# Where the second hidden column's weight sums are computed: in the fill stage, or on three engines in the up stage

## The chip, the cores and the metric

The kernel runs on one core of a Trainium2 chip. The core has TensorE (PE in the profile, with its weight loads as PEld), VectorE (DVE), ScalarE (ACT), GpSimd (POOL) and SyncE (SP), which all run their own instruction queue in order and wait for each other by semaphores. Most loads are issued by SP's queue, most stores by POOL's. The metric is the device time of one execution in microseconds (us). Shown is the median of several runs, and beside it one profiled execution with its trace.

## The reference

One layer of a diffusion backbone, on 1024 latent ("sample") tokens and 128 context ("prompt") tokens of width 1024: a normalised and modulated input goes through a mixer (four GLA heads and four HGRN2 heads, scanned in both directions), an output projection with a gate and a residual, a second norm, and a feed-forward part. The change lies in the first half of the feed-forward part:

```python
def conv_ffn(h, w_up, conv_w, conv_b, w_down, grid):
    u = dw_conv(h @ w_up, conv_w, conv_b, grid)      # 3x3 over the latent grid, width 3 over the prompt
    gate, up = jnp.split(u, 2, axis=-1)
    return (jax.nn.silu(gate) * up) @ w_down
```

`w_up` is 1024 x 5632: 2816 gate channels and 2816 up channels. The outputs are the normed tokens and the final states of the scans.

## The kernel before, in words

*Precision.* Every float32 factor is split into a high part, a copy rounded to `fp32r` made by ScalarE, and a low part, the difference, made by VectorE or GpSimd (`split_lo`, recorded on L69). A product is then three matmuls: high by high, high by low, low by high.

*Stages.* The mixer comes first (to about 724 us). At its end TensorE is filled with the output projection of finished token tiles (L746), whose results go to DRAM (`scr_pre`). Then comes the **fill stage**: the rest of the output projection (`head7` L1486, `heads` L1503), and for each of nine token tiles `mult`, `add`, `square`, `stat` and `norm` (L1411 to L1431), the transposes (L1439, L1460, L1476) and the modulation that makes the feed-forward's token blocks. Then the **up stage** (from about 801 us): 22 hidden columns of 128 gate and 128 up channels each. Then the down product.

*The up product.* For each hidden column c the product of the weights (two rows: gate and up; two halves of the 1024 inputs) with the tokens (two halves of the inputs, two of the tokens) is made by seven block products instead of eight. They need the four weight blocks `11`, `12` (gate), `21`, `22` (up) and four sums of them: `s1` = 21 + 22, `s2` = s1 - 11, `s4` = 12 - s2, `s3` = 11 - 21. A block is 128 x 512. `up(c, p)` (L1921) issues product p: 1 uses `11`, 2 `12`, 3 `s4`, 4 `22`, 5 `s1`, 6 `s2`, 7 `s3`; `up_prompt(c, half)` (L1945) multiplies the prompt with the four blocks themselves. The split weights of all columns live in the tile pair `W` of nine slots, which a search (`plan_slots`, L1690) hands on from column to column. Raw blocks lie in `ra` (`11`, `12`, `21`, `22`) and `sr` (the sums); prompt tokens lie for a while in the last two quarters of `sr`.

From column 2 on, SP loads the raw rows (`load_row`, L1710) a column ahead, GpSimd makes the sums (`weight_sums`, L1732), and ScalarE and GpSimd split them (`split_slots`, L1718). VectorE is left to the convolution of each column (`conv_rows`, L1874, recorded on L1890), which reads the product in PSUM. There are three PSUM tiles `u` of two banks, so a convolution's end sets a later product free.

*Columns 0 and 1 are prepared earlier.* `prepare_up(c)` (L1271) runs for c = 0 and c = 1 behind the mixer: it loads the blocks into the raw buffers, ScalarE copies and VectorE sums and splits, through two `fb` buffers, and GpSimd's queue stores the high and low parts to DRAM (`scr_up`). In the up stage `load_first` (L1763) loads them into `W`.

*Order.* The Tile framework orders each engine's work, and where the text wants an order it writes it by hand: `run(eng, fn)` (L1262) issues `fn` on the engine behind what the last `run` put there. `prepare_up`, the whole fill stage and column 0 go through it, so on VectorE `mult(0)` of the fill stage stands behind the last split of `prepare_up(1)`. The token tiles 0, 1, 4 and 5 are loaded into the raw buffers (`load_xt`, L1391); tile 6's and 7's heads (`load_mh`, L1399) come from DRAM too.

*Tokens in column 0.* While TensorE works on column 0, `prompt_work` (L1797) modulates, copies and splits the prompt, and splits t3; `first_sums` (L1808) makes and splits t4, and adds two products' copies to the gate product, whose convolution starts then.

Of the kernel before, what the change touches and what calls it, by code (L numbers as in the profile page):

```python
# [8 lines left out]
F32 = mybir.dt.float32  # L9
# [3 lines left out]
AF = mybir.ActivationFunctionType  # L13
# [4 lines left out]
P = 128  # L18
# [31 lines left out]
def kernel(ctx: ExitStack, tc: tile.TileContext, ins, outs, stop=None):  # L50
# [46 lines left out]
    scr_up = [[dram.tile([P, 8, 512], F32, name=f"scr_up{c}{x}") for x in "hl"] for c in range(2)]  # L97
    scr_t = [dram.tile([NPAIR, P, 512], F32, name=f"scr_t{i}") for i in range(4)]

    def x_src(t):  # L100
# [1167 lines left out]

    UP0 = ("11", "12", "21", "22", "s1", "s2", "s4", "s3")

    def prepare_up(c):  # L1271

        r = {}
        for row in (1, 2):
            t = rawp.tile([P, 2, 512], F32, name="up0", tag="raw")
            for half in range(2):
                nm = f"{row}{half + 1}"
                r[nm] = t[:, half]
                c0 = (row - 1) * HID + c * P
                nc.sync.dma_start(  # L1280
                    r[nm].rearrange("p (k c) -> p k c", k=4),
                    w_up[half * 512 : (half + 1) * 512, c0 : c0 + P].rearrange("(k p) c -> p k c", p=P),
                )

        def split(nm, place, keep):
            hi = fbp.tile([P, 512], F32R, name="up_hi", tag="fb")
            lo = fbp.tile([P, 512], F32R, name="up_lo", tag="fb") if keep else r[place].bitcast(F32R)
            run("act", lambda: nc.scalar.activation(hi, r[place], AF.Copy))
            run("dve", lambda: split_lo(nc.vector, lo, r[place], hi))
            for i, t in enumerate((hi, lo)):  # L1290
                nc.gpsimd.dma_start(scr_up[c][i][:, UP0.index(nm)], t.bitcast(F32))
# [12 lines left out]
        split("12", "12", True)  # L1304
        in_place("12", "12", "11", ALU.subtract)
        split("s2", "11", False)
        split("s4", "12", False)

    for c in range(2):
        prepare_up(c)  # L1310

    es1.close()
    es_t.close()
# [449 lines left out]
    def load_first(c, nm, dst=None):  # L1763
        for i, x in enumerate("hl"):
            to = dst[x] if dst else W[x][:, SLOT[c][nm]]
            nc.sync.dma_start(flat(to).bitcast(F32), scr_up[c][i][:, UP0.index(nm)])

    def next_weights(c, names):
        if c == 1:
            for nm in names:  # L1770
                load_first(c, nm)
        else:
            split_slots(c, names, nc.gpsimd)

    for nm in ("11", "12"):
        load_first(0, nm, {x: w_slot(0, nm, x) for x in "hl"})
    for nm in ("s1", "s2", "s4", "22", "21", "11", "s3", "12"):
        load_first(0, nm)
    load_row(2, 2)
    load_row(2, 1)  # L1780

    def new_tiles(nm, i):
        for x, j in (("h", 0), ("l", 1)):
# [13 lines left out]
    def prompt_work():  # L1797

        for kt in range(KT):
            modulate_prompt(kt)  # L1800
        copy(0, "p5", u[0][0][:, 512:NS])
        run("act", lambda: nc.scalar.activation(HB["h"]["p"], again["p"], AF.Copy))
        run("dve", lambda: split_lo(nc.vector, HB["l"]["p"], again["p"], HB["h"]["p"]))
        for n in range(2):
            half_hi("t3", n, tmp[n])
            half_lo("t3", n, tmp[n])

    def first_sums():  # L1808

        F = u[0][0]  # L1810
        new_tiles("t4", 1)
        run("dve", lambda: tt(F[:, 0:512], F[:, 0:512], copies["p1"], op=ALU.add))
        for n in range(2):
            token_sum(tmp[2 + n], rb(1, 0, n), tmp[2 + n])
            half_hi("t4", n, tmp[2 + n])
        run("dve", lambda: tt(F[:, 512:NS], F[:, 512:NS], copies["u2"], op=ALU.add))
        for n in range(2):
            half_lo("t4", n, tmp[2 + n])

    token_work()  # L1820
    HB["h"]["p"] = again["late"].tile([P, KT, P], F32R, name="ph", tag="gate")
# [52 lines left out]
    def conv_rows(u, ch, acc, ra=0, rb=NROW):  # L1874

        wc = lambda t: convc[:, t * 44 + ch : t * 44 + ch + 1]
        bc = vcol[:, col["conv_b"] + ch : col["conv_b"] + ch + 1]
        nc.scalar.activation(  # L1878
            acc[:, ra * GRID : rb * GRID], u[:, ra * GRID : rb * GRID], AF.Identity, bias=bc, scale=wc(4)
        )  # L1880
        u3 = u.rearrange("p (r c) -> p r c", c=GRID)
        a3 = acc[:, 0:NS].rearrange("p (r c) -> p r c", c=GRID)
        for dy in (-1, 0, 1):
            for dx in (-1, 0, 1):
                if dy == 0 and dx == 0:
                    continue
                r0, r1 = max(ra, -dy), min(rb, NROW - dy)
                c0, c1 = max(0, -dx), min(GRID, GRID - dx)
                o = a3[:, r0:r1, c0:c1]
                last = nc.vector.scalar_tensor_tensor(  # L1890
                    o,
                    u3[:, r0 + dy : r1 + dy, c0 + dx : c1 + dx],
                    wc(3 * (dy + 1) + dx + 1),
                    o,
                    op0=ALU.mult,
                    op1=ALU.add,
                )
        return last
# [96 lines left out]
    for c in range(NHID + 1):  # L1995
        n = c + 1 if c + 1 < NHID else None
        if c < NHID:
            acc[c] = conv_tiles(c)
            u[c] = [ps_u.tile([P, NS], F32, name="u", tag="u")]

        if c == 0:
            u[0].append(ps_u.tile([P, NS], F32, name="u", tag="u"))
            for p in (1, 2):
                up(0, p)
        if c < NHID:
            up(c, 5)
        if c == 0:
            prompt_work()
        if c > 0:
            prompt_columns(c - 1)  # L2010
            up(c - 1, 4)
            second_half(c - 1)
        if c == NHID:
            break
        if n:
            next_weights(n, ("21", "22"))
            if 2 < n + 1 < NHID:
                load_row(n + 1, 2)
        if c > 0:
            up(c, 2)  # L2020
            up(c, 3)
            u[c].append(ps_u.tile([P, NS], F32, name="u", tag="u"))
            up(c, 1)
        pks[c] = ps_p.tile([P, 2 * P], F32, name="x", tag="x")
        if c > 0:
# [5 lines left out]
        if n:  # L2031
            next_weights(n, ("s1",))
            next_weights(n, ("11", "12"))
            if 2 < n + 1 < NHID:
                load_row(n + 1, 1)
        F, S = u[c]
        if c == 0:
            first_sums()
            up(c, 7)
        else:  # L2040
            nc.vector.tensor_tensor(F[:, 0:512], F[:, 0:512], copies["p1"], op=ALU.add)
            nc.vector.tensor_tensor(F[:, 512:NS], F[:, 512:NS], copies["u2"], op=ALU.add)
        up_prompt(c, 1)
        if c == 0:
            late = again["late"].tile([P, 2304], F32, name="late", tag="mh7")
            ss_t = late[:, 0:2048].rearrange("p (i n) -> p i n", i=4)
            pt_t = late[:, 2048:2304]
        nc.scalar.activation(pt_t, pks[c], AF.Copy)
        if c > 0 and n:
            next_weights(n, ("s2", "s4"))  # L2050
        if c > 0:
            up(c, 7)
        add_s = lambda: nc.vector.tensor_tensor(S[:, 512:NS], S[:, 0:512], copies["p5"], op=ALU.add)
        run("dve", add_s) if c == 0 else add_s()
        anchor["conv"] = conv_rows(F, c, acc[c][0])
        if c == 0:
            next_weights(n, ("s2", "s4"))
        if n:
# [249 lines left out]
```

## Time and profile before

| | us |
|---|---|
| median of three runs | 1571.29 (1568.25 to 1571.6) |
| the profiled execution | 1563.86 |
| its span in the trace | 1562.1 |
| TensorE busy in it | 1486.5 (95%) |
| VectorE / ScalarE / GpSimd busy | 1148.2 / 783.7 / 708.4 |
| mixer's last output products end | 722.8 |
| up stage's first product starts | 800.7 |
| column 1's first product starts | 827.6 |

All places are in us from the start of the span. Rows of a timeline give the start, the duration, the engine, the line and operation, out<-in with the shape, the count, and in brackets the idle time before it and who ended that. Rows of the chain give start, duration and what was on the way to the end; "issue" is time in which the engine waited for nothing that the profile shows. Rows of a wait table give who waited for whom: total, times, longest. Rows of a table by stretches give the stretch and its length, then busy time (and instructions) of PE, PEld, DVE, ACT and POOL, the clock granted to PE, the DMA engines' busy share and GB/s.

### The profile page before, as it was taken

Reading aid. Unit: us, or ns where it says so; the run is one execution under the profiler, and the core shown is the slowest. Engines: PE = TensorE matmul, PEld = TensorE weight load, DVE = VectorE, ACT = ScalarE, POOL = GpSimd, SP = SyncE. Lnnn points to the kernel's source line nnn. Section 1 sums busy time; section 2 is a strip of 40 time slices with the busy share of each in tenths; the row PEclk is TensorE's granted clock in tenths of the full one; section 3 lists DMA queues with packets and bytes.
Section 4 is the critical chain, followed back from the end, with each engine's and each line's share of the span. In section 5 each row is a group of like instructions: output and inputs, shape, how many; then the busy total and the mean of one; then the engine's idle time right before and its main releaser. Section 6 shows DMA issues by size and latency. Waiting matters only on the chain.

```text
span 1562.1 us, 31203 instructions
## 1 busy us (share of the span) xinstructions
PE 1486.5 (95%) x12506; PEld 1255.9 (80%) x12506; DVE 1148.2 (74%) x1739; ACT 783.7 (50%) x1526; POOL 708.4 (45%) x549
## 2 busy tenths in 40 slices
PE   7999999999999989896798999999999999999997
PEld 2699989999898978675687888888888887788886
DVE  3656566664656667645489999999999999579575
ACT  3565667555454555413464444444444444457444
POOL 1412132234232341133215999999999996100001
PEclk9999999999999999998799999999999999999999
DMA  9311112336445452786763465455545567979762
GB/s 341 113 48 47 46 53 63 111 106 214 114 126 164 133 167 86 286 299 234 234 226 140 154 180 135 118 146 135 177 128 135 165 152 218 332 243 360 242 193 116
DMA packets 176524, 260.89 MB, mean 167 GB/s; under 512 B 12244, under 2 KB 114114, under 8 KB 174458
## 3 DMA queue, kind: packets, MB, share of 16 engines
q1 hardware_dynamic: 151895, 176.40, 35.3%
q0 software_dynamic: 23872, 81.80, 16.8%
q8 instruction: 98, 1.61, 0.4%
q10 hardware_dynamic: 611, 0.68, 0.1%
q14 instruction: 48, 0.39, 0.1%
HBM read 194.81 MB, written 87.10 MB: 180 GB/s over the span
## 4 chain that ended last, share of the span: by engine, by line
PE 79%; DMA 6%; DVE 5%; issue 3%; ACT 3%; POOL 3%; SPq 0%; POOLq 0%; ACTq 0%; DVEq 0%
PE u L1743 27%; PE mm L603 13%; PE mm L617 6%; PE xb L2170 6%; PE yb L2170 6%; PE x L1954 4%; PE mm L746 3%; PE lv L935 3%; PE u L1513 2%; PE yb L2221 2%; DVE acc L1890 1%; PE x L1003 1%; PE mm L506 1%; DMA raw<-in_w_in_dram 1%; DMA mh<-scr_m 1%
## 5 line engine op out<-in xcount | busy, mean ns | idle before, releaser
L1890 DVE SCALAR_TENSOR_TENSOR acc<-u,convc,acc 128x945 f32<-128x945 f32 (+2 forms) x352 | 426.7, 1217 | 9.7 <-ACT acc L1878 2.7
L69 POOL TENSOR_TENSOR wl<-raw,wh 128x1024 fp32r<-128x1024 f32 x42 | 103.5, 2466 | 239.5 <-ACT wh L132 183.6
L603 PE MATMUL mm<-h1h,wh 128*128 128x384 f32 x528 | 185.5, 351 | 0.8 <-ACT qj L515 0.8
L603 PE MATMUL mm<-h1l,wh 128*128 128x384 f32 x528 | 179.6, 340 | 0.0
L603 PE MATMUL mm<-h1h,wl 128*128 128x384 f32 x528 | 179.6, 340 | 0.0
L898 DVE TENSOR_TENSOR Q<-Q,fb 128x384 f32<-128x384 f32 x126 | 85.2, 676 | 90.5 <-PE lv L935 88.8
L69 POOL TENSOR_TENSOR wul<-sr,wuh 128x512 fp32r<-128x512 f32 (+1 forms) x62 | 111.8, 1804 | 20.8 <-ACT wuh L1728 20.6
L888 ACT ACTIVATE m<-k 128x384 f32<-128x384 f32 x126 | 70.2, 557 | 87.4 <-PE lv L935 40.5
L69 POOL TENSOR_TENSOR wul<-ra,wuh 128x1024 fp32r<-128x1024 f32 x42 | 107.1, 2550 | 11.8 <-ACT wuh L1728 8.8
L2145 POOL TENSOR_TENSOR sq<-sq,mhalf 128x1 f32<-128x1 f32 x9 | 11.1, 1230 | 211.7 <-DVE sq L2142 211.7
L603 PEld LDWEIGHTS mm<-h1h,wh 128*128 128x128 f32 x528 | 100.0, 189 | 5.7 <-issue 3.9
L603 PEld LDWEIGHTS mm<-h1l,wh 128*128 128x128 f32 x528 | 100.0, 189 | 0.6 <-issue 0.2
L603 PEld LDWEIGHTS mm<-h1h,wl 128*128 128x128 f32 x528 | 99.7, 189 | 0.8 <-issue 0.5
L617 PE MATMUL mm<-wh,h1h 128*128 128x256 f32 x288 | 83.6, 290 | 0.2 <-ACT v L642 0.2
L900 DVE TENSOR_TENSOR k<-k,fb 128x384 f32<-128x384 f32 x126 | 74.1, 588 | 11.3 <-ACT m L888 5.8
L617 PE MATMUL mm<-wh,h1l 128*128 128x256 f32 x288 | 80.4, 279 | 0.0
L617 PE MATMUL mm<-wl,h1h 128*128 128x256 f32 x288 | 80.3, 279 | 0.0
L132 ACT ACTIVATE wh<-raw 128x1024 fp32r<-128x1024 f32 x50 | 52.9, 1058 | 39.4 <-PE mm L603 11.1
L1918 ACT ACTIVATE u2p<-u 128x512 f32<-128x512 f32 x44 | 26.4, 601 | 79.6 <-PE u L1743 79.6
L1986 POOL TENSOR_TENSOR acc<-acc,acc 128x1152 f32<-128x1152 f32 x22 | 60.1, 2730 | 9.7 <-DVE acc L1890 9.7
L1728 ACT ACTIVATE wuh<-ra 128x1024 fp32r<-128x1024 f32 x40 | 42.2, 1055 | 36.8 <-issue 22.1
L1984 ACT ACTIVATE acc<-acc 128x1152 f32<-128x1152 f32 x22 | 25.7, 1170 | 66.5 <-DVE acc L1890 66.5
(385 smaller groups left out, 4529.4 us busy)
## 6 DMA issues: line engine op xcount, KB each, us to landing
ra<-in_w_ffn_up_dram SPq DMA_DIRECT2D x80, 256.0 KB, 3.0
raw<-in_w_in_dram SPq DMA_DIRECT2D x32, 512.0 KB, 4.6
v<-in_w_ada_dram SPq DMA_DIRECT2D x27, 512.0 KB, 4.6
scr_g<-acc POOLq DMA_DIRECT2D x22, 576.0 KB, 5.5
scr_s<-late POOLq DMA_DIRECT2D x11, 1024.0 KB, 5.9
scr_t<-in_w_ffn_down_dram POOLq DMA_DIRECT2D x16, 704.0 KB, 7.2
wa<-in_w_ada_dram SPq DMA_DIRECT2D x16, 512.0 KB, 6.2
scr_t<-in_w_ffn_down_dram POOLq DMA_DIRECT2D x2, 2816.0 KB, 12.9
```

Source lines behind the costliest of these rows:

```text
L69: return eng.tensor_tensor(out, full, hi.bitcast(F32), op=ALU.subtract)
L132: nc.scalar.activation(hi, raw, AF.Copy)
L603: anchor["fill"] = mm(ps, a[:, kt, :], h[kt][b], start=(n == 0), stop=(n == 23))
L617: anchor["fill"] = mm(ps, h[kt][t // 3][:, ts_], a[:, kt % 4, :], start=(n == 0), stop=(n == 23))
L888: nc.scalar.activation(aps(t, 0, [[2 * h, NB], [h, 2], [1, h]]), aps(src, 0, [[2 * h, NB], [BL + h, 2], [1, h]]), AF.Copy)
L898: nc.vector.tensor_tensor(qm, qm, aps(ff_, 2 * h - 1, [[BL - h, 2], [2 * h, NB], [0, h]]), op=ALU.mult)
L900: nc.vector.tensor_tensor(km, km, aps(ff_, BL + 2 * h - 1, [[-(BL + h), 2], [2 * h, NB], [0, h]]), op=ALU.mult)
L1743: last = mm(dst, w_slot(c, a, x)[:, kt, :], HB[y][b][:, kt, :], start=(start and n == 0), stop=(stop and n == 11), skip_group_check=True,)
L1890: last = nc.vector.scalar_tensor_tensor(o, u3[:, r0 + dy : r1 + dy, c0 + dx : c1 + dx], wc(3 * (dy + 1) + dx + 1), o, op0=ALU.mult, op1=AL ...
L1954: last = mm(pk, HB[h]["p"][:, 4 * half + kt, :], aps(flat(W[x]), a * 512 + kt * P, [[(b - a) * 512, 2], [1, P]]), start=(half + kt + n == ...
L1986: last = nc.gpsimd.tensor_tensor(accg, accg, accu, op=ALU.mult)
L2170: anchor["down"] = mm(banks[i], w[a][:, ts_], w[b][:, 512:1024], start=(start and j == 0 and n == 0), stop=(j == NPAIR - 1 and n == 2), sk ...
```

## The change

`prepare_up` runs for column 0 alone; `scr_up` shrinks to one pair. Column 1's raw rows are loaded into `ra` by four SP loads between column 0's loads of `11`, `12` and its others. Its sums and splits are made while column 0 is computed, in this order: VectorE adds `s1` (behind the prompt's split, ahead of t3's); ScalarE and VectorE split `s1` (between t4's two halves on ScalarE, ahead of t4's low part on VectorE); VectorE makes `s2` and `s4`; behind the copy of the prompt's product ScalarE makes the high parts of `11`/`12`, `s2`/`s4` and `21`/`22`, with GpSimd making the low parts; then GpSimd makes `s3`, the rows of column 2 are loaded over column 1's, GpSimd splits `s3` and makes column 2's sums. VectorE's two additions into column 0's gate product move behind t4's low part. In column 1 TensorE takes both prompt products ahead of product 1 (in the other columns from 1 on, one stays behind product 1 and one behind product 6). The prompt's eight scalings (`modulate_prompt`) are on ScalarE in both kernels; no line of the diff touches them.

```diff
-    for c in range(2):
-        prepare_up(c)
+    prepare_up()
...
     for nm in ("11", "12"):
-        load_first(0, nm, {x: w_slot(0, nm, x) for x in "hl"})
+        load_first(nm, {x: w_slot(0, nm, x) for x in "hl"})
+    load_row(1, 2)
+    load_row(1, 1)
     for nm in ("s1", "s2", "s4", "22", "21", "11", "s3", "12"):
-        load_first(0, nm)
-    load_row(2, 2)
-    load_row(2, 1)
+        load_first(nm)
...
         run("dve", lambda: split_lo(nc.vector, HB["l"]["p"], again["p"], HB["h"]["p"]))
+        run("dve", lambda: second_sum("s1", "21", "22", ALU.add, nc.vector))
         for n in range(2):
             half_hi("t3", n, tmp[n])
             half_lo("t3", n, tmp[n])
...
+    def second_sum(to, a, b, op, eng):
+        return eng.tensor_tensor(at(1, to), at(1, a), at(1, b), op=op)
+
+    def second_weights():
+
+        run("pool", lambda: second_sum("s3", "11", "21", ALU.subtract, nc.gpsimd))
+        load_row(2, 2)
+        load_row(2, 1)
+        split_slots(1, ("s3",), nc.gpsimd)
+        weight_sums(2, nc.gpsimd)
+
+    def second_pair(*names):
+        with tc.issue_after(ran["act"].ins):
+            ran["act"], ran["pool"] = split_slots(1, names, nc.gpsimd, both=True)
+
     def first_sums():
 
         F = u[0][0]
-        new_tiles("t4", 1)
-        run("dve", lambda: tt(F[:, 0:512], F[:, 0:512], copies["p1"], op=ALU.add))
         for n in range(2):
             token_sum(tmp[2 + n], rb(1, 0, n), tmp[2 + n])
-            half_hi("t4", n, tmp[2 + n])
-        run("dve", lambda: tt(F[:, 512:NS], F[:, 512:NS], copies["u2"], op=ALU.add))
+        new_tiles("t4", 1)
+        half_hi("t4", 0, tmp[2])
+        slot = SLOT[1]["s1"]
+        hi, lo = (flat(W[x][:, slot]) for x in "hl")
+        raw = flat(at(1, "s1"))
+        run("act", lambda: nc.scalar.activation(hi, raw, AF.Copy))
+        run("dve", lambda: split_lo(nc.vector, lo, raw, hi))
+        half_hi("t4", 1, tmp[3])
+        run("dve", lambda: second_sum("s2", "s1", "11", ALU.subtract, nc.vector))
+        run("dve", lambda: second_sum("s4", "12", "s2", ALU.subtract, nc.vector))
         for n in range(2):
             half_lo("t4", n, tmp[2 + n])
+        run("dve", lambda: tt(F[:, 0:512], F[:, 0:512], copies["p1"], op=ALU.add))
+        run("dve", lambda: tt(F[:, 512:NS], F[:, 512:NS], copies["u2"], op=ALU.add))
...
         if c > 0:
             up(c, 2)
             up(c, 3)
+        pks[c] = ps_p.tile([P, 2 * P], F32, name="x", tag="x")
+        if c == 1:
+            up_prompt(c, 0)
+            up_prompt(c, 1)
+        if c > 0:
             u[c].append(ps_u.tile([P, NS], F32, name="u", tag="u"))
             up(c, 1)
...
-        nc.scalar.activation(pt_t, pks[c], AF.Copy)
+        copy_pt = lambda: nc.scalar.activation(pt_t, pks[c], AF.Copy)
+        if c == 0:
+            run("act", copy_pt)
+            second_pair("11", "12")
+            second_pair("s2", "s4")
+            second_pair("21", "22")
+        else:
+            copy_pt()
...
         if c == 0:
-            next_weights(n, ("s2", "s4"))
-        if n:
-            next_weights(n, ("s3",))
+            ran["act"] = anchor["rows"]
+            second_weights()
+        elif n:
+            split_slots(n, ("s3",), nc.gpsimd)
             if n + 1 < NHID:
                 weight_sums(n + 1, nc.gpsimd)
```

More of the change, by code (lines that the diff above doesn't have):

```diff
@@ L96 @@
     scr_s = [dram.tile([P, 4, 512], F32, name=f"scr_s{j}") for j in range(NPAIR)]
-    scr_up = [[dram.tile([P, 8, 512], F32, name=f"scr_up{c}{x}") for x in "hl"] for c in range(2)]
+    scr_up = [dram.tile([P, 8, 512], F32, name=f"scr_up{x}") for x in "hl"]
     scr_t = [dram.tile([NPAIR, P, 512], F32, name=f"scr_t{i}") for i in range(4)]
@@ L1269, with prepare_up @@
     UP0 = ("11", "12", "21", "22", "s1", "s2", "s4", "s3")
-    def prepare_up(c):
+    def prepare_up():
         r = {}
@@ L1278, in prepare_up @@
                 r[nm] = t[:, half]
-                c0 = (row - 1) * HID + c * P
+                c0 = (row - 1) * HID
                 nc.sync.dma_start(
@@ L1290, in split @@
             for i, t in enumerate((hi, lo)):
-                nc.gpsimd.dma_start(scr_up[c][i][:, UP0.index(nm)], t.bitcast(F32))
+                nc.gpsimd.dma_start(scr_up[i][:, UP0.index(nm)], t.bitcast(F32))
         def in_place(to, a, b, op):
@@ L1761, in w_slot, with load_first @@
         return W[x][:, SLOT[c][nm]]
-    def load_first(c, nm, dst=None):
+    def load_first(nm, dst=None):
         for i, x in enumerate("hl"):
[L1765 to L1773, printed above, removed]
+            to = dst[x] if dst else W[x][:, SLOT[0][nm]]
+            nc.sync.dma_start(flat(to).bitcast(F32), scr_up[i][:, UP0.index(nm)])
     for nm in ("11", "12"):
-        load_first(0, nm, {x: w_slot(0, nm, x) for x in "hl"})
+        load_first(nm, {x: w_slot(0, nm, x) for x in "hl"})
+    load_row(1, 2)
+    load_row(1, 1)
     for nm in ("s1", "s2", "s4", "22", "21", "11", "s3", "12"):
-        load_first(0, nm)
-    load_row(2, 2)
-    load_row(2, 1)
+        load_first(nm)
     def new_tiles(nm, i):
@@ L1877, in conv_rows @@
         bc = vcol[:, col["conv_b"] + ch : col["conv_b"] + ch + 1]
-        nc.scalar.activation(
+        anchor["rows"] = nc.scalar.activation(
             acc[:, ra * GRID : rb * GRID], u[:, ra * GRID : rb * GRID], AF.Identity, bias=bc, scale=wc(4)
@@ L2014 @@
             break
-        if n:
-            next_weights(n, ("21", "22"))
-            if 2 < n + 1 < NHID:
+        if c and n:
+            split_slots(n, ("21", "22"), nc.gpsimd)
+            if n + 1 < NHID:
                 load_row(n + 1, 2)
@@ L2021 @@
             up(c, 3)
+        pks[c] = ps_p.tile([P, 2 * P], F32, name="x", tag="x")
[3 more added lines that the diff above has]
+        if c > 0:
             u[c].append(ps_u.tile([P, NS], F32, name="u", tag="u"))
             up(c, 1)
-        pks[c] = ps_p.tile([P, 2 * P], F32, name="x", tag="x")
-        if c > 0:
+        if c > 1:
             up_prompt(c, 0)
@@ L2030 @@
             up_prompt(c, 0)
[L2031 to L2034, printed above, removed]
+        if c and n:
+            split_slots(n, ("s1",), nc.gpsimd)
+            split_slots(n, ("11", "12"), nc.gpsimd)
+            if n + 1 < NHID:
                 load_row(n + 1, 1)
@@ L2042 @@
             nc.vector.tensor_tensor(F[:, 512:NS], F[:, 512:NS], copies["u2"], op=ALU.add)
-        up_prompt(c, 1)
+        if c != 1:
+            up_prompt(c, 1)
         if c == 0:
@@ L2047 @@
             pt_t = late[:, 2048:2304]
-        nc.scalar.activation(pt_t, pks[c], AF.Copy)
+        copy_pt = lambda: nc.scalar.activation(pt_t, pks[c], AF.Copy)
[6 more added lines that the diff above has]
+            copy_pt()
         if c > 0 and n:
-            next_weights(n, ("s2", "s4"))
+            split_slots(n, ("s2", "s4"), nc.gpsimd)
         if c > 0:
@@ L2056 @@
         if c == 0:
-            next_weights(n, ("s2", "s4"))
-        if n:
-            next_weights(n, ("s3",))
+            ran["act"] = anchor["rows"]
+            second_weights()
+        elif n:
+            split_slots(n, ("s3",), nc.gpsimd)
             if n + 1 < NHID:
```

## The prediction

> **What bounds the kernel now.** I read the page's share lines first, then the chain, then the PE and SP queues around the step that is moved.
>
> ```profile
> span 1562.1 us, 31203 instructions
> PE 1486.5 (95%) x12506; PEld 1255.9 (80%) x12506; DVE 1148.2 (74%) x1739; ACT 783.7 (50%) x1526; POOL 708.4 (45%) x549
> ```
>
> TensorE bounds the whole, so a change is worth what it does to TensorE's gaps. Only two places in the prepared weights' life show large gaps. The first is the start of the fill stage (TensorE's and then the chain's rows, start and duration first, idle time before in brackets):
>
> ```profile
> 724.97 0.71 PE L1494 MATMUL u<-wh,mh 128*128 128x512 f32 x2 [2.20 <-DMA wh<-scr_wo]
> ...
> 728.70 0.61 PE L1494 MATMUL u<-wh,mh 128*128 128x512 f32 x2
> 739.43 1.22 PE L1494 MATMUL u<-wh,mh 128*128 128x512 f32 x2 [10.12 <-DVE xn L1413]
> ...
> 745.85 0.61 PE L1494 MATMUL u<-wh,mh 128*128 128x512 f32 x2
> 756.04 1.22 PE L1513 MATMUL u<-wh,mh 128*128 128x512 f32 x2 [9.57 <-DVE xn L1413]
> ```
>
> ```profile
> 736.89 0.64 ACT up_hi L1288
> ...
> 737.55 0.04 DVE up L69
> ...
> 738.16 1.23 DVE xn L1413
> 739.41 1.24 DVE xt L1416
> ...
> 747.60 5.91 DMA xt<-scr_pre
> ...
> 753.63 1.23 DVE xt L1416
> 754.85 1.15 DVE xn L1413
> ...
> 756.04 8.61 PE u L1513 x24
> ...
> 771.44 4.14 PE u L1513 x18
> ```
>
> The first three head products end at 729.3. The fourth needs a PSUM tile that the multiply `mult(0)` (L1413) frees. `run` has put that multiply behind the last split of `prepare_up(1)` (L1288 and L69), so it starts at 738.16, though its input was there by about 726.4 (six of the 18 matmuls). The second gap waits for `mult(3)`, which stands behind `add(1)`, which waits for its token tile. SyncE's waits from 700 to 830 us (total, times, longest) say why that load went so late:
>
> ```profile
> SPq L1766 <- PE u L1513: 10.9, 2, 8.5
> ...
> SPq L1397 <- DMA scr_up1l<-up: 9.2, 2, 5.4
> SPq L1404 <- DMA scr_up1h<-up_hi: 7.1, 1, 7.1
> ```
>
> The token loads (L1397) wait for the raw buffers of `prepare_up(1)`, and the head loads (L1404) for its stores out of the `fb` buffers, all in one SP queue. Both gaps belong to the step that the change takes away.
>
> The second place is the start of hidden column 1:
>
> ```profile
> 827.58 0.77 PE L1743 MATMUL u<-t1h,wuh 128*128 128x512 f32 x1 [5.92 <-DMA wuh<-scr_up1h]
> ```
>
> ```profile
> 821.39 4.54 DVE L69 TENSOR_TENSOR t4l<-acc,t4h 128x1024 fp32r<-128x1024 f32 x2 [0.52 <-ACT t4h L1381]
> ...
> 826.46 7.52 DVE L1890 SCALAR_TENSOR_TENSOR acc<-u,convc,acc 128x945 f32<-128x945 f32 x6
> ...
> 836.89 1.20 DVE L1890 SCALAR_TENSOR_TENSOR acc<-u,convc,acc 128x945 f32<-128x945 f32 x1 [0.17 <-ACT acc L1878]
> ...
> 843.72 0.70 DVE L2041 TENSOR_TENSOR u<-u,cp 128x512 f32<-128x512 f32 x1 [0.27 <-ACT cp L1918]
> ...
> 851.12 1.20 DVE L1890 SCALAR_TENSOR_TENSOR acc<-u,convc,acc 128x945 f32<-128x945 f32 x1 [2.51 <-ACT acc L1878]
> ```
>
> ```profile
> 866.80:889.34 22.54, 22.54 (x112) 18.64 (x111) 21.82 (x24) 10.46 (x14) 21.62 (x15) 1.00 0.52 166
> ```
>
> The last row (PE, PEld, DVE, ACT, POOL busy) is one later column: PE, DVE and POOL are all full. So a gap of PE in column 1 is gained only as far as VectorE also gets ahead.
>
> **The change, part by part.**
>
> *Fill stage, what goes.* `prepare_up(1)`: eight SP loads, eight ScalarE copies, eight VectorE splits and four sums, sixteen stores on POOL's queue. Upper bound: both gaps, 10.12 + 9.57 = 19.69 us, and the slow matmuls behind them. The 18 matmuls behind the first gap took 739.43 to 746.46, 7.03 us, against 724.97 to 729.31, 4.34 us, for the same 18 before it: 2.69. The 24 from 756.04 took 8.61 against 24 x 4.14/18 = 5.52: 3.09. Together 25.5 us.
>
> *What is late next.* VectorE needs these steps before `heads(6)`: `mult(0)`, `add(0)`, `mult(1)`, `mult(2)`, `add(1)`, `mult(3)`, six at 1.15 us (start to start, 753.63 and 754.85 with 1.23 duration less overlap), and one small `stat`, 0.1. From 726.4 that gives 733.4. TensorE alone, with six warm heads from 724.97, gives 724.97 + 2 x 4.34 = 733.65. So at best `heads(6)` starts at 733.6 instead of 756.04, and warm. Then the transfers:
>
> ```profile
> DMA packets 2359, 7.96 MB, mean 295 GB/s; under 512 B 352, under 2 KB 352, under 8 KB 2358
> ...
> 717.80:725.00 7.20, 5.00 (x26) 3.93 (x24) 6.01 (x12) 1.91 (x7) 3.50 (x6) 1.00 0.86 269
> 725.00:730.00 5.00, 4.32 (x18) 3.24 (x18) 1.16 (x2) 1.68 (x3) 2.05 (x4) 1.00 1.05 408
> ...
> 745.00:750.00 5.00, 1.47 (x6) 0.81 (x5) 0.00 (x0) 0.00 (x0) 0.00 (x0) 0.84 1.06 275
> ```
>
> The first row is 718 to 745; in the others the last two columns are DMA share and GB/s. The DMA engines are full from 725 on at 408 GB/s, and at 275 with the narrow head loads. Ahead of `heads(6)` must come two pairs of output weights (2 MB), modrB (0.25), four token tiles (2) and tile 6's heads (0.9), by the tiles' shapes in the code: 5.15 MB, 4.25/0.408 + 0.9/0.275 = 13.7 us from 717.8, so 731.5, if only these are under way. Tile 7's heads (0.9 MB, 3.3 us) may be in between: 734.8, and a landing after that. I take 735.5 for `heads(6)`, 2 us under the best. Later loads and stores move closer together as well: at no cost if the queue order suits, at most the 6 us of one more late tile (5.91); I take 1.5. Fill term: 25.5 - 2 - 1.5 = 22 less.
>
> *Eight scaling instructions of the prompt.* Line 1482 is on ScalarE in the kernel before already, and no line of the diff touches it: 0.
>
> *Row loads.* Four SP loads of column 1's rows now stand between column 0's four weight loads (to 789.6) and the sixteen others (798.2):
>
> ```profile
> 789.21 0.43 SPq L1766 DMA_DIRECT2D w<-scr_up0l  x1
> 798.22 0.32 SPq L1766 DMA_DIRECT2D wuh<-scr_up0h  x1
> ...
> 812.38 2.79 SPq L1713 DMA_DIRECT2D ra<-in_w_ffn_up_dram  x4
> ```
>
> They took 2.79 us of SP, and the queue waits 8.5 us there for TensorE. They are free, provided their tile is. By the sizes in the code `ra` lies on the former constants and raw buffers (2,400 + 2 x 4,096 bytes a partition), whose last reader is `norm(5)`, well ahead of 789:
>
> ```profile
> 773.56 1.15 ACT L1431 ACTIVATE xn<-xt,acc 128x1024 f32<-128x1024 f32 x1 [0.29 <-POOL acc L1426]
> ```
>
> Cost 0; what it costs if the cover goes is the second rival. Sixteen loads of column 1's split weights (SP, 815 to 826) go: that is PE's 5.92 us gap.
>
> *Column 0 and 1, VectorE.* Four ops of 512 columns (sums s1, s2, s4 and s1's split) come in, 4 x 0.6 = 2.4 us start to start, and two of the same length move behind t4's split, which leaves it 1.2 us later by count. Against that the pair of 4.54 us was stretched:
>
> ```profile
> 815.05 2.35 DVE L69 TENSOR_TENSOR t3l<-acc,t3h 128x1024 fp32r<-128x1024 f32 x2
> ```
>
> The same pair without POOL took 2.35: POOL's sums for column 2, L1734 to L1737, ran beside the slow one. They move behind column 1's weights, so 2.2 us come back unless POOL's new splits hit the same pair. t4's low part is then ready between 824.9 and 827.3 (before 825.9), and column 0's convolution, behind the two moved sums and ScalarE's 1.2 us start of it, starts between 827.3 and 829.7 (before 826.46). From its start to column 1's (851.12) are 24.66 us with 0.17 + 0.27 + 2.51 = 2.95 of idle, which PE's earlier start fills, since TensorE no longer waits for weights: 21.7 us of work. Column 1's convolution comes at 849.0 to 851.4: 0.3 later to 2.1 earlier. I take 1 us gained, and not 5.92: VectorE does not let PE keep more.
>
> *Column 1's weights on POOL.* Three pairs of 1024 columns, then s3's sum and split.
>
> ```profile
> 821.38 1.26 POOL L1737 TENSOR_TENSOR sr<-ra 128x512 f32<-128x512 f32 x1
> 822.61 2.24 POOL L1735 TENSOR_TENSOR sr<-sr,ra 128x512 f32<-128x512 f32 x1
> ...
> 835.84 2.40 POOL L69 TENSOR_TENSOR wul<-ra,wuh 128x1024 fp32r<-128x1024 f32 x1 [8.78 <-ACT wuh L1728]
> 845.26 1.30 POOL L69 TENSOR_TENSOR wul<-sr,wuh 128x512 fp32r<-128x512 f32 x1 [7.02 <-ACT wuh L1728]
> ```
>
> From 823.5 they end at 825.9, 828.3 and 830.7; products 2 and 3 and the prompt's want them at about 828, 831 and 834, that is 2 to 3 us of slack each. POOL's idle 8.78 + 7.02 = 15.8 us in column 1 takes the 7.2 + 2.6 and column 2's sums (5.2) behind a 3 us load: 18 us from 823.5, 841.5, with column 2's s1 due by 848. Cost 0, at most 3 if every op is stretched like the 2.24.
>
> The Trainium skill, SBUF — State Buffer, section "SBUF: two separate sides", speaks against this part: a VectorE instruction with two SBUF inputs and a GpSimd one exclude each other for the whole instruction. The stretched 4.54 agrees. By the rule t4's last half could wait one whole POOL split, and column 1 would gain nothing: 22 in place of 23 in the sum.
>
> **Sum.** 22 + 1 = 23 us less. The profiled execution took 1563.86 us (span 1562.1), so it would take 1541. The three runs' median is 1571.29, 7.4 above it; against that, which is what a new median stands beside, 1548.3. About 0.2%, 3 us, is what this kernel's runs can tell from no change.
>
> **The rivals.**
> *Transfers take the gap over.* For it: the full DMA rows from 725 to 750. Against it: eight loads and sixteen stores of the moved step drop out. If SP keeps the before's order, with all six first head loads ahead of `add(1)`'s tile, that order took 742.93 to 753.5, 10.6 us; begun at 725.9, behind the second pair of weights, it lands at 736.5, `heads(6)` follows at 739, 17 us earlier; a late tile after it (5.91) leaves 12 with column 1's 1: 1559.
> *Slower: the row loads block.* SP is in order, and the s1 sum stands ahead of t3, t4 and all convolutions on VectorE. If `ra` came free late, sixteen loads of column 0 would queue behind it. They take 798.2 to 812.0; the first product that needs one begins at 806.17, so some 3 us can be lost unseen. The loads may start by 795.4 (798.2 less 2.8) at no cost; from a release 23 + 3 us later (821) this outweighs the gain; 10 us beyond that it is 1581. `norm(5)` at 773.6 speaks against it.
> *No change.* The wait could go to a fill-stage step that I count as hidden, by chance of the same size; I see no row for it.
>
> **Chances.** Forecast (15 to 28 us gained) 0.66; transfers (4 to 15 gained) 0.19; no change 0.03; slower, by row loads or an order on the queues that I don't see, 0.12. Faster 0.85, same 0.03, slower 0.12. The likeliest case alone is 1543 to 1556. The range adds the transfers' case, to 1564, and 2 us below for the runs' own spread (1568.25 to 1571.6): 1541 to 1564.
>
> **What would show it.** In the profile after: no `up` work between 703 and 742; TensorE's idle between 722 and 757 under 6 us in place of 22, and `heads(6)` near 735; the row loads at SP about 765 without a wait; the first product of column 1 without a DMA wait; DVE's idle before column 1's convolution gone. Wrong it would be with a new wait for xt or mh in the fill stage, for `ra`, or for a POOL split ahead of column 1's products.

## The result, and the profile after

The changed kernel took 1549.99 us (median of four runs, 1547.47 to 1550.51) against 1571.44 for the kernel before on the same chip: 21.5 us less, a ratio of 0.9863 with a 95% interval of 0.9844 to 0.9882. On another chip, against 1569.51, the same kernel took 1546.87, ratio 0.9855 (0.9834 to 0.9875). The forecast was 1548.3.

The page of the kernel after begins so:

```profile
span 1548.1 us, 31132 instructions
PE 1487.8 (96%) x12506; PEld 1255.0 (81%) x12506; DVE 1145.5 (74%) x1731; ACT 783.2 (51%) x1523; POOL 708.9 (46%) x538
```

TensorE's work is the same, 1487.8 us against 1486.5, so the time came out of its gaps. These are its rows at the places of the prediction (timeline, idle time and who ended it in brackets):

```profile
729.10 0.70 PE L1493 MATMUL u<-wh,mh 128*128 128x512 f32 x2 [1.23 <-DMA wh<-scr_wo]
...
738.12 0.73 PE L1512 MATMUL u<-wh,mh 128*128 128x512 f32 x2 [0.55 <-DVE xn L1412]
...
745.16 0.66 PE L1438 MATMUL x<-ident,xn 128*128 128x128 f32 x4 [1.08 <-ACT xn L1430]
...
798.58 0.50 PE L1742 MATMUL u<-t3l,wuh 128*128 128x512 f32 x1 [0.42 <-DVE t3l L69]
811.01 0.79 PE L1742 MATMUL u<-t4h,wuh 128*128 128x512 f32 x1 [5.05 <-DVE u L2081]
828.59 0.50 PE L1742 MATMUL u<-t2h,wuh 128*128 128x512 f32 x1 [1.04 <-ACT cp L1934]
833.08 0.50 PE L1742 MATMUL u<-t3h,wuh 128*128 128x512 f32 x1 [1.47 <-ACT u2p L1934]
```

In the fill stage the gap of 10.12 us ahead of the fourth head product is gone, that of 9.57 us ahead of `heads(6)` has become 0.55, and 1.08 us ahead of a transpose are new. But the gap of 5.92 us for column 1's weights has a successor: 5.05 us ahead of column 0's product 4 (t4), which TensorE takes behind column 1's first product. Two smaller ones follow in column 1.

A single pair of spans hides part of this, because the mixer ahead of all that was changed takes a few us more or less from one execution to the next. So I cut the span at five instructions: the first matmul of the output projection (L746), the first head product (`head7`), the first up product, and the first matmul of product 5 in columns 2 and 3. "Again" is the same kernel on another chip.

| us | before | before again | after | after again |
|---|---|---|---|---|
| to the first output matmul | 640.4 | 643.4 | 645.4 | 643.5 |
| from there to the first head product | 84.5 | 83.6 | 83.7 | 83.4 |
| fill stage | 75.8 | 75.4 | 52.2 | 52.1 |
| first up product to column 2 | 50.5 | 51.1 | 54.7 | 54.4 |
| column 2 to column 3 | 22.4 | 22.4 | 22.3 | 22.3 |
| column 3 to the end | 688.5 | 688.4 | 689.8 | 689.6 |
| span | 1562.1 | 1564.3 | 1548.1 | 1545.4 |

The fill stage gives 23.5 us, the start of the up stage takes 3.7 back. The first row differs by up to 3 us between two executions of one kernel. From column 3 to the end the kernel after takes 1.2 us more, where two executions of one kernel differ by 0.2 only; over all profiles of this study that stretch takes 688.0 to 691.3 us. No edit touches it, and the 1.2 us stay open.

### The profile page after: what moved, and what is told of

Its sections match the earlier page's. It is cut to its first block, busy times and chain, and to the rows that moved or that the text cites. A ratio compares the mean times of both kernels' runs of the same rounds, so it can differ in the third digit from the quotient of the medians.

```text
span 1548.1 us, 31132 instructions
## 1 busy us (share of the span) xinstructions
PE 1487.8 (96%) x12506; PEld 1255.0 (81%) x12506; DVE 1145.5 (74%) x1731; ACT 783.2 (51%) x1523; POOL 708.9 (46%) x538
## 4 chain that ended last, share of the span: by engine, by line
PE 78%; DMA 6%; DVE 6%; issue 4%; ACT 3%; POOL 2%; SPq 1%; POOLq 0%; ACTq 0%; DVEq 0%
PE u L1742 26%; PE mm L603 13%; PE xb L2199 6%; PE yb L2199 6%; PE mm L617 5%; PE x L1970 4%; PE mm L746 3%; PE lv L935 3%; PE yb L2250 2%; PE u L1512 2%; DVE acc L1906 2%; PE x L1003 1%; PE mm L506 1%; DMA mh<-scr_m 1%; DMA wa<-in_w_ada_dram 1%
## 5 line engine op out<-in xcount | busy, mean ns | idle before, releaser
L69 POOL TENSOR_TENSOR wul<-sr,wuh 128x512 fp32r<-128x512 f32 (+1 forms) x64 | 116.2, 1816 | 19.5 <-ACT wuh L1727 19.3
L69 POOL TENSOR_TENSOR wul<-ra,wuh 128x1024 fp32r<-128x1024 f32 x44 | 112.3, 2552 | 20.3 <-ACT wuh L1727 17.8
L1727 ACT ACTIVATE wuh<-ra 128x1024 fp32r<-128x1024 f32 x42 | 44.3, 1055 | 39.5 <-issue 16.6
L1727 ACT ACTIVATE wuh<-sr 128x512 fp32r<-128x512 f32 (+1 forms) x62 | 48.1, 775 | 24.1 <-PE x L1970 16.1
```

Source lines behind the costliest of these rows:

```text
L69: return eng.tensor_tensor(out, full, hi.bitcast(F32), op=ALU.subtract)
L1727: first = nc.scalar.activation(hi, raw, AF.Copy)
```

## The experiments

Two theories of the fill stage stood against each other: that removing the second preparation gives the gain there, and that the gain came from elsewhere. Then, what about the preparation was so dear: its work, its stores, or the chain of both. For the up stage: what the 3.7 us are, and whether they can be had back.

**The fill stage alone.** The kernel before, without the second preparation.

```diff
-    for c in range(2):
-        prepare_up(c)
+    prepare_up(0)
...
-            nc.sync.dma_start(flat(to).bitcast(F32), scr_up[c][i][:, UP0.index(nm)])
+            nc.sync.dma_start(flat(to).bitcast(F32), scr_up[0][i][:, UP0.index(nm)])
```

> The kernel before without prepare_up for column 1; column 1 loads the stored weights of column 0, so its product is computed with the wrong weights, and all other work is the same. Theory (the gain is the fill stage's two gaps): from the first head product to the first up product 52 us, as after, in place of 75.8; the 5.9 us gap ahead of column 1 stays, and the time is 20 to 26 us under the kernel before. Rival (the gain comes from the new order in the up stage, or from the mixer): the fill stage stays over 65 us and the time is within 8 us of the kernel before.

Measured 1546.63 us against 1569.36, 22.7 less (ratio 0.9846, 0.982 to 0.9872).

TensorE's rows of this kernel:

```profile
738.04 0.73 PE L1512 MATMUL u<-wh,mh 128*128 128x512 f32 x2 [0.56 <-DVE xn L1412]
...
807.45 0.77 PE L1742 MATMUL u<-t1h,wuh 128*128 128x512 f32 x1 [5.32 <-DMA wuh<-scr_up0h]
```

The fill stage is 52.1 us, as after, and the wait for column 1's weights (5.32, TensorE's rows above) stays. From the first up product to column 2 it takes 49.9 us, like the kernel before. So the whole gain is the removal, and the way the sums come back adds nothing to it: this kernel has the old up stage and gains as much as the change. By the stretches it should gain 4 us more; the times (22.7 less here, 21.5 and 22.6 for the change) do not show that.

**The old work back in the fill stage.** The kernel after, with column 0's preparation run twice.

```diff
     prepare_up()
+    prepare_up()
```

> The kernel after with the preparation of column 0 done twice, so that the fill stage has the old work back and the up stage is as after. Theory: fill stage 74 to 78 us; as the up stage of the kernel after is some 3 us longer to column 1's convolution than that of the kernel before (53.8 against 50.4), the time is 0 to 6 us above the kernel before. Rival (up stage gains as forecast, 1 us): 1 to 3 us under it.

Measured 1573.02 against 1569.36: ratio 1.0021 (1.0006 to 1.0037), 3.7 us slower (about 1 to 6 by the interval). The fill stage is 74.6 us, and TensorE's gaps are back:

```profile
746.31 1.22 PE L1494 MATMUL u<-wh,mh 128*128 128x512 f32 x2 [9.09 <-DVE xn L1413]
762.49 1.22 PE L1513 MATMUL u<-wh,mh 128*128 128x512 f32 x2 [9.06 <-DVE xn L1413]
...
835.65 0.79 PE L1743 MATMUL u<-t4h,wuh 128*128 128x512 f32 x1 [5.02 <-DVE u L2082]
```

The new up stage is thus a loss of some 4 us by itself, as the theory has it, and not the forecast's gain of 1: from the first up product to column 2 this kernel takes 54.6 us, like the kernel after.

**Which part of the preparation.** First without the sixteen stores, then with the transfers and without the copies, sums and splits.

```diff
-            for i, t in enumerate((hi, lo)):
-                nc.gpsimd.dma_start(scr_up[c][i][:, UP0.index(nm)], t.bitcast(F32))
+            if c == 0:
+                for i, t in enumerate((hi, lo)):
+                    nc.gpsimd.dma_start(scr_up[c][i][:, UP0.index(nm)], t.bitcast(F32))
```

> The kernel before with the second preparation's loads, copies, sums and splits, but without its sixteen stores; column 1 loads column 0's weights. Theory A (the preparation is slow because each copy waits until a store has emptied its buffer): its last split is done by 720, both gaps are under 4 us together, the fill stage takes 52 to 56 us, and the time is 18 to 24 us under the kernel before. Theory B (the copies and splits themselves are what VectorE's order waits for): the last split stays after 730 and less than 10 us are gained.

```diff
         def split(nm, place, keep):
+            if c == 1:
+                for i in range(2):
+                    nc.gpsimd.dma_start(scr_up[c][i][:, UP0.index(nm)], r[place])
+                return
...
         def in_place(to, a, b, op):
+            if c == 1:
+                return
```

> The kernel before with the second preparation's loads and its sixteen stores (of the raw blocks, unsplit), without its copies, sums and splits; column 1 loads column 0's weights. If the 4 MB of stores and their place on POOL's queue are the cost, less than 10 us are gained and the token tiles stay late. If only the chain copy, store, next copy is, the stores go out back to back behind the loads and land by 720, the fill stage takes 52 to 57 us, and 17 to 24 us are gained.

Without stores 1552.79 (16.6 less; 0.989, 0.9864 to 0.9915), fill stage 58.6 us. With transfers alone 1557.31 (12.1 less; 0.9914, 0.9887 to 0.9941), fill stage 60.1. Both lie between the numbers that were expected. The rows say why. In the kernel before, ScalarE's copy waits until a store has emptied its buffer (a row of the chain, just ahead of the copy at 736.89):

```profile
734.35 2.44 DMA scr_up1l<-up_lo
```

Without stores, the last copies start at 724.68, not by 720, and the first gap is gone, since `mult(0)` waits only for TensorE. ScalarE's row of the last copies, kernel without stores:

```profile
724.68 1.16 ACT L1288 ACTIVATE up_hi<-up 128x512 fp32r<-128x512 f32 x2
```

VectorE's rows of the same kernel:

```profile
734.31 1.23 DVE L1414 TENSOR_TENSOR xn<-u,gate 128x1024 f32<-128x1024 f32 x1 [2.19 <-PE u L1495]
...
747.20 1.23 DVE L1417 TENSOR_TENSOR xt<-xn,xt 128x1024 f32<-128x1024 f32 x1 [5.11 <-DMA xt<-scr_pre]
```

A later token tile is still 5.11 us late. SP waits 9.2 us for a raw buffer that VectorE's split holds; that keeps back the first token tile's load, to 723.10, and all loads behind it in SP's queue. The late tile's own load waits for no buffer, but goes out among the others at 736.29 and takes 10.81 us to land, where those of the kernel after take 3.9 to 6.6 (the three whose landing the profile shows). The DMA engines are full then (1.06 and 1.10 from 730 to 742). SP's wait, and the load in the chain:

```profile
SPq L1398 <- DVE up L69: 9.2, 1, 9.2
```

```profile
736.29 10.81 DMA xt<-scr_pre
```

With transfers alone it is again the tile that is late. VectorE's row of that kernel, and two rows of its chain:

```profile
746.71 1.22 DVE L1422 TENSOR_TENSOR xt<-xn,xt 128x1024 f32<-128x1024 f32 x1 [6.11 <-DMA xt<-scr_pre]
```

```profile
731.52 9.94 DMA scr_up1l<-up
...
741.53 5.06 DMA xt<-scr_pre
```

Here the tile's load waits until the store of a raw block has landed. So neither the stores nor the engines' work is the cost alone. The work and the stores together make the first gap (stores off or work off, it goes), and either of them holds the raw buffers long enough for a token tile to be late, directly or through the loads that pile up behind. Taking one away gives 12 to 17 of 23 us.

**The up stage: three edits of the kernel after.** First, the last addition of column 0 ahead of t4's low part.

```diff
             first_sums()
             up(c, 7)
+            run("dve", lambda: nc.vector.tensor_tensor(S[:, 512:NS], S[:, 0:512], copies["p5"], op=ALU.add))
+            late_sums()          # t4's low part and the two gate additions
...
-        run("dve", add_s) if c == 0 else add_s()
+        if c > 0:
+            add_s()
```

> The kernel after, with column 0's last addition (product 7 plus p5, which reads the PSUM columns that product 4 adds to) ahead of t4's low part on VectorE instead of behind both gate additions. Theory (product 4 waits for that addition): TensorE's gap ahead of product 4 shrinks from 5.05 to 3 to 4 us, to the end of t4's split; the convolution starts as before it, so the whole gains 0 to 1.5 us on the kernel after. Rival (the gap is t4's split alone): 5 us stay.

Second, s1's split early.

```diff
-        for n in range(2):
-            token_sum(tmp[2 + n], rb(1, 0, n), tmp[2 + n])
-        new_tiles("t4", 1)
-        half_hi("t4", 0, tmp[2])
         slot = SLOT[1]["s1"]
...
         run("act", lambda: nc.scalar.activation(hi, raw, AF.Copy))
+        token_sum(tmp[2], rb(1, 0, 0), tmp[2])
         run("dve", lambda: split_lo(nc.vector, lo, raw, hi))
+        token_sum(tmp[3], rb(1, 0, 1), tmp[3])
+        new_tiles("t4", 1)
+        half_hi("t4", 0, tmp[2])
         half_hi("t4", 1, tmp[3])
```

> The kernel after, with s1's copy ahead of t4's halves on ScalarE and its split between the two token sums on VectorE. Theory (the idle 1.65 us, and t4's split meeting POOL's first pair, 4.51 in place of 2.35, delay column 0's convolution): both go, t4's pair takes 2.4 to 2.9 us, column 0's convolution starts 30.4 - 4 = 26.5 us after the first up product in place of 30.4, and 3 to 4 us are gained on the kernel after. Rival (VectorE's order is not what sets the end): the convolution starts earlier and less than 1 us is gained.

Third, the prompt products of column 1 where the other columns have them.

```diff
-        if c == 1:
-            up_prompt(c, 0)
-            up_prompt(c, 1)
...
-        if c > 1:
+        if c > 0:
             up_prompt(c, 0)
...
-        if c != 1:
-            up_prompt(c, 1)
+        up_prompt(c, 1)
```

> The kernel after, with column 1's two prompt products back behind products 1 and 6. Theory: they delayed product 1's copy, for which VectorE waited 1.70 us; that wait goes and 0.5 to 2 us are gained. Rival (they cover the wait for a PSUM tile or for a weight pair): TensorE gets a new wait ahead of product 1 or of a prompt product, and nothing is gained or 1 to 3 us are lost.

Measured against 1566.03 on their chip: 1546.97 (0.9877, 0.9862 to 0.9892), 1542.95 (0.9859, 0.984 to 0.9878) and 1545.37 (0.9871, 0.9854 to 0.9888). These ratios overlap with that of the kernel after, so the times alone do not rank them; the stretch from the first up product to column 2 does: 55.2, 50.2 and 52.0 us, against 54.7 and 54.4 after.

The early addition was a miss. Product 4's first matmul no longer waits, but the second, the first that needs t4's low part, does: 5 us stay, as the rival has it. The gap is t4's late split, not the place of the addition. TensorE's row, VectorE's and then GpSimd's, kernel with the early addition:

```profile
807.86 0.80 PE L1742 MATMUL u<-t4l,wuh 128*128 128x512 f32 x1 [5.23 <-DVE t4l L69]
```

```profile
801.38 6.42 DVE L69 TENSOR_TENSOR t4l<-acc,t4h 128x1024 fp32r<-128x1024 f32 x2
```

```profile
801.05 2.40 POOL L69 TENSOR_TENSOR wul<-ra,wuh 128x1024 fp32r<-128x1024 f32 x1 [17.78 <-ACT wuh L1727]
803.39 3.34 POOL L69 TENSOR_TENSOR wul<-sr,wuh 128x1024 fp32r<-128x1024 f32 x1
806.68 3.36 POOL L69 TENSOR_TENSOR wul<-ra,wuh 128x1024 fp32r<-128x1024 f32 x1
```

0.6 us later, both halves of t4's split wait for a GpSimd split: 6.42 us in place of 4.51. In the kernel with s1 early the split comes first (it ends at 801.74, GpSimd's first pair begins at 801.48 and takes 2.49), column 0's convolution starts 26.8 us after the first up product, not 30.4, and TensorE's wait ahead of product 4 is 1.23 us, though the addition stands where it stood. VectorE's rows, GpSimd's and then TensorE's, kernel with s1 early:

```profile
799.39 2.35 DVE L69 TENSOR_TENSOR t4l<-acc,t4h 128x1024 fp32r<-128x1024 f32 x2
...
804.77 1.20 DVE L1906 SCALAR_TENSOR_TENSOR acc<-u,convc,acc 128x945 f32<-128x945 f32 x1 [0.30 <-ACT acc L1894]
```

```profile
801.48 2.49 POOL L69 TENSOR_TENSOR wul<-ra,wuh 128x1024 fp32r<-128x1024 f32 x1 [17.87 <-ACT wuh L1727]
```

```profile
803.73 0.50 PE L1742 MATMUL u<-t4h,wuh 128*128 128x512 f32 x1 [1.23 <-DVE u L2081]
```

That is the theory's 4 us, with column 2 4.2 to 4.5 us earlier. The edit takes away VectorE's idle time and the meeting with GpSimd together, so what each is worth alone is not shown. The prompt order brought 2.4 to 2.7 in this stretch, more than the 0.5 to 2 expected: VectorE's wait of 1.70 us is gone. In the stretch its only price is a wait of 0.20 us ahead of product 1; but from column 3 to the end this profile takes 691.3 us, 1.5 more than those of the kernel after, and its time shows no gain. TensorE's row of the kernel with the prompt order:

```profile
818.58 0.50 PE L1742 MATMUL u<-b11h,wuh 128*128 128x512 f32 x1 [0.20 <-DVE acc L1906]
```

**Together, with the kernel after on the same chip.** s1 early and the prompt order; these two and the early addition; the kernel after.

> The kernel after with both edits that helped alone: s1's split early, and column 1's prompt products back behind products 1 and 6. If the two gains add (from the first up product to column 2's: 54.7 us after, 50.2 with s1 early, 52.0 with the prompt's order), 47.5 to 49 us and 5 to 8 us under the kernel after. If both fill the same slack of VectorE, 50 us and 3 to 5 us under it.

> The same two edits, and the last addition ahead of t4's low part. With the addition in front t4's pair comes 0.6 us later and meets POOL's first split again: if that decides, t4's pair takes 3.5 to 6 us again and the kernel is 1 to 3 us slower than with the two edits; if TensorE's wait for the addition (1.23 us with s1 early) decides, it is 0.5 to 1 us faster.

> The kernel after once more, as the measure for the two others on the same chip: ratio to the kernel before 0.984 to 0.988, fill stage 52 us, column 2 at 54 to 55 us behind the first up product.

Measured against 1569.51: 1543.11 (0.9826, 0.9801 to 0.985), 1543.68 (0.9835, 0.9818 to 0.9852), and 1546.87 for the kernel after. The four runs of the first two (1538.50 to 1545.73, 1543.50 to 1545.40) do not touch those of the kernel after (1546.44 to 1548.44): by the medians 3 to 4 us faster than the kernel after, and 26 us faster than the kernel before. Column 2 comes 49.9 and 50.7 us after the first up product. With s1 early alone it was 50.2, so the gains do not add; they fill the same slack. TensorE now reaches product 1 early and waits there for VectorE's convolution to set a PSUM tile free. The first row is the kernel with two edits, the second that with all three:

```profile
820.80 0.50 PE L1742 MATMUL u<-b11h,wuh 128*128 128x512 f32 x1 [2.92 <-DVE acc L1906]
```

```profile
819.42 0.76 PE L1742 MATMUL u<-b11h,wuh 128*128 128x512 f32 x1 [5.03 <-DVE acc L1910]
```

With all three, t4's pair took 2.35 us: it came ahead of GpSimd's split, which waited instead, so the slow pair that one side expected did not come back. Nor did a gain: the stretch is 0.8 us longer than with the two edits, the medians are 0.6 us apart, within their spread.

**The kernel before once more.**

> The kernel before once more, unchanged, for its profile: how far the mixer and the other stages differ from one execution to the next. The first profile of it was 7 us under the median and had its first head product at 724.97, the kernel after 729.10. If that is chance, this one is at 727 to 731 and its fill stage is again 75 to 77 us.

1566.06 us, fill stage 75.4, first head product at 726.98, the lower end of what was expected. The stretch up to 640 us, which no edit touches, put the first output matmul between 640.4 and 647.6 in all profiles of this study. A difference of a few us between two spans has to be looked for stage by stage.

## Why the prediction was right, and where it was not

The total (23 us less forecast, 21.5 and 22.6 measured) is right, and so is its main cause, but two of its terms missed in opposite directions, so that the number lies so near is in part luck.

*First gap, VectorE's order: right.* `mult(0)` now waits 0.81 us, and for TensorE. Its and the next rows of VectorE:

```profile
730.76 1.23 DVE L1412 TENSOR_TENSOR xn<-u,gate 128x1024 f32<-128x1024 f32 x1 [0.81 <-PE u L1493]
732.02 1.23 DVE L1415 TENSOR_TENSOR xt<-xn,xt 128x1024 f32<-128x1024 f32 x1
...
736.85 1.22 DVE L1412 TENSOR_TENSOR xn<-u,gate 128x1024 f32<-128x1024 f32 x1
```

*Second gap, the transfers: right in kind, charged too much.* `heads(6)` starts 9.0 us after the first head product. The step gave 8.6 at best and took 10.5, with 1.5 more for later loads; the fill stage gained 23.5 where 22 stood. I had all transfers start at 717.8. SP's rows show that with the buffers free two token tiles and the loads of both first heads go out 10 to 26 us ahead of the weights' reload (722.90):

```profile
697.14 0.33 SPq L1396 DMA_DIRECT2D xt<-scr_pre  x1
706.96 2.62 SPq L1403 DMA_DIRECT2D mh<-scr_m  x4
709.69 0.44 SPq L1396 DMA_DIRECT2D xt<-scr_pre  x1
710.45 2.59 SPq L1403 DMA_DIRECT2D mh<-scr_m  x4
722.90 0.33 SPq L147 DMA_DIRECT2D wl<-scr_wo  x1
```

The DMA engines are as full as was feared, 1.03 at 420 GB/s from 729 to 734, but no engine waits for a load in the fill stage from there on. The rival "transfers take the gap over" falls with that, in this kernel; the two halves of the preparation show it alive, with a late token tile in both.

*Slow matmuls: right.* They are gone behind both former gaps: the heads at 738.12 begin with 0.73 us for a pair, where it was 1.22, and the granted clock is 1.00 from 722.9 to 781, where it was 0.84 from 745 to 750 before.

*Row loads: right.* They go out at 770.29 without a wait of their own, and SP still waits 4.1 us for TensorE behind them. The slower rival falls.

*Column 1's weights on POOL: right for TensorE.* No product waits for a split. What they cost shows on VectorE.

*Column 0 and 1 on VectorE: wrong, 3.7 us lost where 1 gained was taken.* The step added VectorE's four new operations up start to start (2.4 us) and gave their inputs no wait. But s1's split needs ScalarE's copy of s1, which stands behind t4's first copy, and that copy waits for both token sums, because the new tile lies over the rows that both sums read. A row of before already said so: ScalarE's copies began at 820.30, behind the second sum. ScalarE's row of before, and two after:

```profile
820.30 2.01 ACT L1381 ACTIVATE t4h<-acc 128x1024 fp32r<-128x1024 f32 x2 [4.05 <-DVE acc L1378]
```

```profile
800.83 1.06 ACT L1380 ACTIVATE t4h<-acc 128x1024 fp32r<-128x1024 f32 x1 [4.05 <-DVE acc L1377]
801.79 0.62 ACT L1826 ACTIVATE wuh<-sr 128x512 fp32r<-128x512 f32 x1
```

So s1's copy was late, VectorE stood idle 1.65 us, and t4's split came to lie on GpSimd's first pair. VectorE's and then GpSimd's rows after:

```profile
802.44 0.69 DVE L69 TENSOR_TENSOR wul<-sr,wuh 128x512 fp32r<-128x512 f32 x1 [1.65 <-ACT wuh L1826]
...
804.38 4.51 DVE L69 TENSOR_TENSOR t4l<-acc,t4h 128x1024 fp32r<-128x1024 f32 x2
...
811.69 1.20 DVE L1906 SCALAR_TENSOR_TENSOR acc<-u,convc,acc 128x945 f32<-128x945 f32 x1 [0.49 <-ACT acc L1894]
...
828.57 0.70 DVE L2061 TENSOR_TENSOR u<-u,cp 128x512 f32<-128x512 f32 x1 [1.70 <-ACT cp L1934]
```

```profile
804.65 3.15 POOL L69 TENSOR_TENSOR wul<-ra,wuh 128x1024 fp32r<-128x1024 f32 x1 [17.79 <-ACT wuh L1727]
```

The convolution starts 30.4 us after the first up product; it was 25.7 before, and the step had 26.6 to 29.0 (its upper end, 827.3, is 827.1 by its own terms). TensorE's gap ahead of product 4 follows from the same lateness. Product 4 also has a dependence that the step left out: it adds into the PSUM columns that column 0's last addition (L2081) reads, and that addition had come to stand behind t4's split and two others. The row names it, but it is not what costs: with the addition moved ahead 5.23 us stay, and with s1 early, the addition in its place, 1.23. From column 0's convolution to the next the step had 21.7 us without idle. It took 23.4: VectorE idled 1.70 us ahead of product 1's copy, and with the prompt products in their usual places that wait is gone. Of the two, the late t4 is the larger: s1's early split gave 4.2 to 4.5 us back alone, the prompt order 2.4 to 2.7, both together hardly more than the first (49.9 us against 50.2).

The Trainium skill's rule (SBUF — State Buffer, section "SBUF: two separate sides") that a VectorE instruction with two SBUF inputs and a GpSimd one exclude each other agrees with the runs: t4's pair took 2.35 us when neither half waited, 4.51 when one did, 6.42 when both did. I had weighed it at 1 us. It is why the 2.2 us that the step hoped for did not come back; it is not what made the up stage slower than before, for t4's pair took 4.54 us there too.

*The sum against the runs.* 22 + 1 stand against 23.5 - 3.7 = 19.8 from the stages, 18.6 with the 1.2 us from column 3 to the end; the medians say 21.5 and 22.6. The 3 to 4 us between are not explained: the mixer ahead of the change differs as much between two executions of one kernel.

## What to carry to other kernels

A step that is put ahead of others "where engines have room" can cost what its buffers and its place in the order hold up, and not only what it keeps busy: the first thing to read is who waits for the engine behind its last instruction, and which loads wait for its buffers. When a wait goes, look in the trace for every instruction that had finished under its cover, also for what reads a result that the next product overwrites. And a dependence that the trace names need not be what costs: move it, and see whether the gap goes. Before two engines are set to work side by side, check that they do not exclude each other; taking one small split 2.9 us earlier on VectorE gave back more than 4 us here.

## What the runs showed of the hardware that was not expected

One VectorE split pair of 2 x 1024 columns, beside GpSimd splits of 1024, took 2.35, 4.51 or 6.42 us as none, one or both of its halves waited, and a GpSimd split that waited took 3.13 to 3.36 in place of 2.40. The convolution's instructions, which read one operand from PSUM, keep to 1.20 us beside the same GpSimd splits.

In the up stage TensorE's matmuls behind a gap of 5.02 us and more began slow (0.76 to 0.80 us for the first); the granted clock was 0.55 from 811 to 817 in the kernel after. Behind 2.92 us, in the kernel with s1 early and the prompt order, the first took 0.50, but 1.5 us on six took 0.58 to 0.63, at a granted clock of 0.50 from 823 to 825:

```profile
822.30 0.58 PE L1742 MATMUL u<-b11h,wuh 128*128 128x512 f32 x1
822.68 0.63 PE L1742 MATMUL u<-b11l,wuh 128*128 128x512 f32 x1
```

Behind 2.45 us, with s1 early, the clock stayed at 1.00 (825 to 831). The Trainium skill (TensorE: Matmul & The Clock Gate, section "What's actually happening") gives an idle window of about 3.4 us for the lower clock. The gap of 2.92 us is shorter and was followed by it all the same, so here the measurement decides.
